# Chunk outputs of a state-space layer straight from the inputs by row-tiled products, without a filter table in DRAM, and the key rows in other accumulator banks than the queries'

## The chip, the core and the metric

The kernel runs on one core of a Trainium2 chip as one program. The metric is the device time of an execution in microseconds. Five engines work side by side, each through its own queue in order: TensorE (PE, its weight loads PEld), VectorE (DVE), ScalarE (ACT), GpSimd (POOL) and SyncE (SP), which here issues DMAs.

## The reference

Two transformer blocks in float32 on 256 tokens of width 1024, with 16 meta tokens ahead of them (272 rows) in the first block. The change touches the first layer's first half alone:

```python
proj = rms_norm(h, norm1_g) @ w_in                  # q 512, k 128, v 128, u 512
attn = sliding_window_attention(q, k, v, ...)       # 8 query heads, 2 key heads, window 128, meta, sinks
ssm  = s5_ssm(u, ...)                               # 32 groups of 16 channels, 64 complex states each
h = h + concat(rms_norm(attn), rms_norm(ssm)) @ w_out
```

`s5_ssm` is a diagonal linear recurrence: s_t = a s_(t-1) + B u_t and y_t = Re(C s_t) + d u_t, then z = gelu(y) and z * sigmoid(z @ glu_w + glu_b). After this half comes the expert layer with product keys (8 heads, 16 of 16384 experts each), and then the second block, with two more layers.

## The kernel before

The program is written as a flow of Python generators over tiles; a planner at compile time puts the instructions of each engine in order by its own estimates, their place in the program and the dependencies. A call `c.after(b, a)` tells it that b must stand behind a on its engine. Each tile of a pool has a tag; tiles of one tag share one buffer (or as many as `bufs` says), and the next tile waits until all uses of the last are over.

PSUM has eight banks in this half: `p` twice, `y`, `o`, `m` twice, `b` twice. Every product of w_in and w_out runs as three fp32r products (`mm3`: high by high, high by low, low by high; lines 1702 to 1704). The weights come through a feed: SP loads a unit of 512 KB into one of five buffers (L89), ScalarE casts the high part (H, L102), and VectorE subtracts to give the low part (Lo, L103; GpSimd for the first four units).

The order of the first half: the rows are normalized and transposed, u is projected into the banks p, p, y, o, and `enter` copies it out by ScalarE (uP), writes it to DRAM (udr) and reads it back as U, 8 steps by 16 channels on 128 partitions. `powers` makes the tables W (six VectorE operations on 2048 columns, ending at L452), `tables` makes rotation tables on GpSimd, and `outputs` makes the output tables G (six VectorE operations on 2304 columns, L590 to L595). Their temporaries share buffers: `tg` has the buffers t0 and t1, and the state inputs st later take t0.

Then two things run interleaved. In the background `kv` projects keys and values (banks p, p, o), normalizes the key rows by 13 small VectorE operations (rstd) and scales them into ks (L285); `q` projects the queries (banks p, p, eight steps of six products); `attention` computes 16 scores (L363, two for each head), adds the mask (L364), takes exponentials (L372), transposes the weights (L392), multiplies by the values (L401, L405) and projects with the first half of w_out. In the foreground `Ssm.run` works in chunks of 8 steps (SJ = 8, 34 chunks):

1. `maps` transposes W into WT (L561). 32 fp32 products of U by WT (L633; each fp32 product is two instructions) give the chunk inputs to the states, which ScalarE copies into st (L638).
2. `response` multiplies bd by G (32 products on four column tiles, L608) to the impulse response K of 8 steps, 16 by 16 for each group. K with zeros in front goes to DRAM (kdr, L616), and eight DMAs (L620) read it back shifted, as a table T of 128 by 128 for each group.
3. VectorE rotates the state inputs (L647 to L650), scans over the chunks (L655), rotates back (L658, L659) and writes S (L667).
4. The chunk outputs, four blocks b of four pairs j of groups, in the banks y, b, y, b:

```python
m = nc.tensor.matmul(y[q:q + 32, o], self.U[:, 2 * j + g, 2:], self.T[:, 2 * j + g], ...)     # L689, g = 0, 1
m = nc.tensor.matmul(y[0:64, o], S[z][:, j]..., self.G[z][:, j, 1:]..., ...)                  # L695, z = 0, 1
```

5. GELU on ScalarE (L699), transposes to zT (L705), and the GLU product (L718), whose weights (`glu`, 1 MB, L351) are loaded once the buffers of the first stage are free.

After step 3 GpSimd zeroes 2048 columns and sends them to `wscr` by four DMAs of 2 MB (L672), behind the last read of T. Two orders by hand bear on the feed: units 11 to 14 (w_out) are loaded behind the last read of T, unit 10 behind the reads of U. The attention weights' transposes stand behind the last L695 (`ylast`). When both halves of the flow are done, `ssm_glu` applies the gate (tanh, L742; L744 to L748) and the second half of w_out follows; then the expert layer begins.

Of the kernel before, what the change touches and what calls it, by code (L numbers as in the profile page):

```python
# [19 lines left out]
FT = mybir.dt.float32  # L20
# [36 lines left out]
CST = {}  # L57
NCST = _cols(CST, [("ident", 128), ("iota", 128), ("bd", 8), ("ones", 1), ("g2", 8), ("tok", 1)])

# [118 lines left out]
def first_half(c):  # L178
# [4 lines left out]
    with ExitStack() as ctx:  # L183
# [50 lines left out]

        up = [c.psum(t) for t in ("p", "p", "y", "o")]
        for k in range(3):
# [14 lines left out]
        ssm.tables()  # L251
        ssm.outputs()

# [9 lines left out]
        def kv():  # L263
            ps = [c.psum(t) for t in ("p", "p", "o")]
            for q in range(2):
                H, Lo = c.feed.take()
                for k2 in range(4):
                    k = 4 * q + k2
                    for i, s, m in ((0, slice(16, 144), 128), (1, slice(144, 272), 128), (2, slice(0, 16), 16)):
                        n = slice(k2 * 256, k2 * 256 + 256)  # L270
                        c.mm3(ps[i][:m, :256], hH[:, k, s], hL[:, k, s], H[:, n], Lo[:, n], k == 0, k == 7)
                    yield 980
            kss = inp.tile([128, 3, 2], FT, name="kss")
            ks = inp.tile([128, 3, 128], FT, name="ks")
            vm = inp.tile([16, 128], FT, name="vm")
            rep = inp.tile([16, 8, 16], FT, name="rep")
            V.memset(kss, 1.0)
            V.tensor_copy(rep, c.ident[:16, None, :16].to_broadcast([16, 8, 16]))
            for i, m in ((0, 128), (1, 128), (2, 16)):
                nc.scalar.activation(ks[:m, i], ps[i][:m, :128], AF.Square)  # L280
                V.tensor_reduce(kss[:m, i], ks[:m, i].rearrange("p (h d) -> p h d", h=2), axis=AX.X, op=OP.add)
                nc.scalar.copy(vr[:, i] if i < 2 else vm, ps[i][:m, 128:256])
            kr = c.rstd(kss.rearrange("p a b -> p (a b)"), 6, 1.0 / 64)
            for i, m in ((0, 128), (1, 128), (2, 16)):
                V.tensor_tensor(ks[:m, i].rearrange("p (h d) -> p h d", h=2), ps[i][:m, :128].rearrange("p (h d) -> p h d", h=2),  # L285
                                kr[:m, 2 * i:2 * i + 2, None].to_broadcast([m, 2, 64]), op=OP.mult)

            def turn():
                p = c.psum("m")
                nc.tensor.transpose(p[:, 0:16], ks[:16, 2], c.ident[:16, :16])  # L290
                for i in range(2):
                    nc.tensor.transpose(p[:, 16 + i * 128:144 + i * 128], ks[:, i], c.ident)
                nc.scalar.activation(kT, p[:, :L], AF.Copy, scale=P1("kg"))

            def spread():
# [137 lines left out]
class Ssm:  # L433
# [106 lines left out]
    def enter(self, up):  # L540

        nc, c, one = self.nc, self.c, self.one
        uP = one.tile([128, 4 * L], FT, tag="uP", name="uP").rearrange("p (a j c) -> p a j c", a=4, j=SJ)
        self.U = U = one.tile([128, 32, SC], FT, name="U")
        for ct in range(4):
            nc.scalar.copy(uP[:, ct].rearrange("p j c -> p c j"), up[ct][:, :L].rearrange("p (c j) -> p c j", j=SJ))
            nc.sync.dma_start(c.udr[ct * 128:(ct + 1) * 128], uP[:, ct])
        src = c.udr.rearrange("(g q) j c -> q j g c", q=16)
        for j in range(SJ):
            m = SJ - 1 - j  # L550
            self.had = [nc.sync.dma_start(U[16 * m:16 * m + 16], src[:, j])]
# [29 lines left out]
    def outputs(self):  # L581
# [8 lines left out]
        for op in (V.tensor_tensor(self.G[0], C[0], a[0], op=OP.mult), V.tensor_tensor(t[0], C[1], a[1], op=OP.mult)):  # L590
            c.after(op, self.wdone)
        V.tensor_tensor(self.G[0], self.G[0], t[0], op=OP.subtract)
        c.after(V.tensor_tensor(self.G[1], C[0], a[1], op=OP.mult), self.wdone)
        V.tensor_tensor(t[1], C[1], a[0], op=OP.mult)
        V.scalar_tensor_tensor(self.G[1], self.G[1], -1.0, t[1], op0=OP.mult, op1=OP.subtract)  # L595

    def response(self, left):


        nc, c, V, P1, one = self.nc, self.c, self.V, self.P1, self.one  # L600
        K = one.tile([128, 4 * L], FT, tag="uP", name="K")[:, :4 * (2 * SJ - 1) * 16].rearrange("p (a m q) -> p a m q", a=4, q=16)
        V.memset(K[:, :, :SJ - 1], 0.0)
        p = c.psum("m")
        for j in range(16):
            q = 32 * (j % 4)
            o = p[q:q + 32, (j // 4) * 128:(j // 4) * 128 + 128]
            for z in range(2):
# [3 lines left out]
                last = m  # L611
        yield
        p4 = p.rearrange("p (a m q) -> p a m q", a=4, m=SJ)
        V.tensor_tensor(K[:, :, SJ - 1], p4[:, :, 0], P1("dk").rearrange("p (a q) -> p a q", a=4), op=OP.add)
        nc.scalar.copy(K[:, :, SJ:], p4[:, :, 1:])
        nc.sync.dma_start(c.kdr.rearrange("(a p) n -> p a n", p=128), K.rearrange("p a m q -> p a (m q)"))  # L616
        self.T = one.tile([128, 4096], FT, tag="T", name="T").rearrange("p (g n) -> p g n", g=32)
        src = c.kdr.rearrange("(g q) n -> q g n", q=16)
        for m in range(SJ):
            t = nc.sync.dma_start(self.T[16 * m:16 * m + 16], src[:, :, 16 * m:16 * m + 128])  # L620
        self.had.append(t)

    def run(self, glu, out):
        nc, c, V, one = self.nc, self.c, self.V, self.one
        yield 8000
        self.maps()

        st = self.temp("s", 0)[:, :2 * 16 * SC].rearrange("p (z j c) -> p z j c", z=2, j=16)
        for j0, n in ((0, 6), (6, 5), (11, 5)):
# [9 lines left out]
            yield 0  # L639
        respond = self.response(left)  # L640
        next(respond)

# [7 lines left out]
        V.tensor_tensor(m1[:, 1], m1[:, 1], m2[:, 0], op=OP.subtract)  # L650
        next(respond, None)
        yield 2000
# [18 lines left out]
        for i in range(4):  # L671
            m = nc.gpsimd.dma_start(c.wscr[:, 32 * i:32 * i + 32].rearrange("p b t -> p (b t)").rearrange("p (a n) -> p a n", n=2048),  # L672
                                    zero[:, None, :].to_broadcast([128, 2, 2048]))
            c.after(m, self.had[1])
        yield 2000
# [5 lines left out]
        for b in range(4):  # L681
            y = c.psum("yb"[b % 2])
            prev = None
            for jj in range(4):
                j = 4 * b + jj
                o = slice(128 * jj, 128 * jj + 128)
                for g in range(2):
                    q = 32 * g
                    m = nc.tensor.matmul(y[q:q + 32, o], self.U[:, 2 * j + g, 2:], self.T[:, 2 * j + g], start=(jj == 0), stop=False,  # L689
                                         tile_position=(0, q), skip_group_check=True)  # L690
                    if prev is not None:
                        c.after(m, prev)
                    prev = m
                for z in range(2):
                    m = nc.tensor.matmul(y[0:64, o], S[z][:, j].rearrange("p g c -> p (g c)"), self.G[z][:, j, 1:].rearrange("p a b -> p (a b)"),  # L695
                                         start=False, stop=(z == 1), skip_group_check=True)
            self.ylast = m
# [4 lines left out]
        for h in range(2):  # L702
            p = c.psum("by"[h])
            for i in range(SJ):
# [5 lines left out]

        for u, i in [(10, 0)] + [(u, 1) for u in range(11, 15)]:
            if u < len(c.feed.issued):
# [930 lines left out]
def body(tc, A, out):  # L1643
# [3 lines left out]
    with ExitStack() as ctx:  # L1647
# [80 lines left out]
        c.udr = tc.dram_tile([512, SJ, SC], FT, name="udr")  # L1728
        c.kdr = tc.dram_tile([512, (2 * SJ - 1) * 16], FT, name="kdr")
        c.ascr = [tc.dram_tile([128, AB, T], FT, name="ascr%d" % i) for i in range(NB // AB)]  # L1730
# [53 lines left out]
def layout(inp):  # L1784
# [18 lines left out]

    cp = np.arange(512).reshape(2, 8, 2, 16).transpose(0, 2, 1, 3).reshape(-1)
    wo = np.concatenate([wo[:512][qp], wo[512:][cp]], 0)
# [15 lines left out]
    for p in range(16):  # L1821
# [19 lines left out]
           (i // 16 == np.arange(8)[None]).astype(f),  # L1841
           np.ones((128, 1), f), col(g["norm2_g"][0], 8), np.arange(128, dtype=f)[:, None]]
    A["pk1"] = np.concatenate(p1 + [z, causal, z, prev, causal], 1)
# [54 lines left out]
```

## Time and profile before

| | us |
|---|---|
| median of 3 runs (lowest, highest) | 1330.38 (1329.16, 1342.03) |
| the profiled execution: time | 1329.63 |
| the profiled execution: span of the trace | 1327.9 |
| TensorE busy | 1260.6 (95%) |
| VectorE busy | 935.7 (70%) |
| ScalarE busy | 648.7 (49%) |
| GpSimd busy | 292.9 (22%) |
| mean granted clock of TensorE | 0.977 of full |

The profile is that of one execution. An engine's busy share is a mean over stages with different limits: the expert layer and the second block fill most of the span, and the stage that the change touches lies in the first 190 us. A row of a timeline has the start, the length from the first start to the last end, the engine, the line, the operation with output and inputs, and the count; in brackets stands the engine's idle time before it and what ended it. The granted clock is 1.00 at 2.4 GHz and 0.50 at 1.2 GHz.

### The profile page before, as it was taken

The numbers are of one execution on the slowest core, as the hardware profiler recorded it, in microseconds if no ns is written. First come the engines' busy times: TensorE is split into PE (matmuls) and PEld (weight loads), VectorE is DVE, ScalarE is ACT, GpSimd is POOL, SyncE is SP. The second block draws the span as 40 slices with busy tenths as digits, with TensorE's granted clock in tenths as the row PEclk, the third lists the DMA queues.
The fourth block names the chain that finished last, engine by engine and source line by source line (L and its number), as shares of the span: only waits on it lengthen the run. The fifth ranks groups of instructions, "written<-read, shape, count | busy, mean of one in ns | idle before, by whom it ended". The sixth has DMA issues, their size and how long they took to land.

```text
span 1327.9 us, 21246 instructions
## 1 busy us (share of the span) xinstructions
PE 1260.6 (95%) x7816; PEld 1092.6 (82%) x7816; DVE 935.7 (70%) x2193; ACT 648.7 (49%) x1119; POOL 292.9 (22%) x201
## 2 busy tenths in 40 slices
PE   4569999999999999999899999999999999999998
PEld 4556789999999999999788788888887778777776
DVE  6973368898988666665588875555557795678854
ACT  4424345545545444444454444444446647455562
POOL 7010000377877777720000000000000001000010
PEclk9886979999999999999899999999999999999999
DMA  5349255688888777798799986656667454563231
GB/s 201 70 58 357 99 168 191 206 224 225 221 232 228 183 203 203 201 354 303 256 309 312 310 266 190 190 188 187 187 187 239 123 162 141 173 219 112 80 113 46
DMA packets 106296, 262.75 MB, mean 198 GB/s; under 512 B 31552, under 2 KB 37056, under 8 KB 103888
## 3 DMA queue, kind: packets, MB, share of 16 engines
q1 hardware_dynamic: 75280, 227.77, 54.9%
q0 software_dynamic: 21696, 16.85, 7.0%
q10 hardware_dynamic: 9216, 16.78, 3.4%
q8 instruction: 61, 1.00, 0.3%
q14 instruction: 43, 0.35, 0.1%
HBM read 232.72 MB, written 28.38 MB: 197 GB/s over the span
## 4 chain that ended last, share of the span: by engine, by line
PE 84%; DVE 6%; ACT 2%; DMA 1%; issue 1%; DVEq 0%; SPq 0%; ACTq 0%
PE ps L890 26%; PE ps L1702 10%; PE ps L1703 10%; PE ps L1704 10%; PE pr L1702 5%; PE pr L1704 5%; PE pr L1703 5%; PE ps L1103 2%; PE m L1295 2%; DVE Lo L103 2%; PE o L1340 2%; PE m L363 1%; PE m L1334 1%; DMA ga<-ascr 1%; ACT H L102 1%
## 5 line engine op out<-in xcount | busy, mean ns | idle before, releaser
L102 ACT CAST H<-w 128x1024 fp32r<-128x1024 f32 (+1 forms) x370 | 386.2, 1045 | 502.3 <-PE ps L1703 193.2
L103 DVE TENSOR_TENSOR Lo<-w,H 128x1024 fp32r<-128x1024 f32 (+1 forms) x366 | 445.2, 1218 | 186.8 <-ACT H L102 186.5
L1702 PE MATMUL ps<-xH,H 128*128 128x256 f32 x1024 | 290.9, 284 | 0.0
L1703 PE MATMUL ps<-xL,H 128*128 128x256 f32 x1024 | 287.8, 281 | 0.0
L1704 PE MATMUL ps<-xH,Lo 128*128 128x256 f32 x1024 | 287.6, 281 | 0.0
L1061 POOL DMA_INDIRECT wscr<-sent x128 | 238.6, 1864 | 219.6 <-DVE act L1038 153.8
L890 PE MATMUL ps<-H,a 128*128 128x512 f32 x1024 | 281.9, 397 | 4.8 <-ACT a L902 3.0
L890 PEld LDWEIGHTS ps<-H,a 128*128 128x128 f32 x1024 | 194.2, 190 | 50.9 <-ACT a L902 3.2
L1702 PEld LDWEIGHTS ps<-xH,H 128*128 128x128 f32 x1024 | 193.1, 189 | 0.0
L1703 PEld LDWEIGHTS ps<-xL,H 128*128 128x128 f32 x1024 | 193.1, 189 | 0.0
L1704 PEld LDWEIGHTS ps<-xH,Lo 128*128 128x128 f32 x1024 | 192.9, 188 | 0.0
L890 PE MATMUL ps<-Lo,a 128*128 128x512 f32 x512 | 161.4, 397 | 0.3 <-DVE Lo L103 0.3
L1382 POOL TENSOR_TENSOR emx<-emx,vz 128x512 f32<-128x512 f32 x2 | 3.5, 1750 | 543.7 <-DVE vz L1228 543.7
L890 PEld LDWEIGHTS ps<-Lo,a 128*128 128x128 f32 x512 | 96.9, 189 | 23.4 <-DVE Lo L103 0.9
L900 DVE TENSOR_TENSOR act<-ga,act 128x256 f32<-128x256 f32 x128 | 47.5, 420 | 25.8 <-DMA ga<-ascr 25.8
L1702 PE MATMUL pr<-H,exH 128*128 128x512 f32 x128 | 52.5, 410 | 1.3 <-ACT exH L1143 1.0
L903 DVE TENSOR_TENSOR a<-act,a 128x256 fp32r<-128x256 f32 x128 | 53.5, 419 | 0.0
L902 ACT CAST a<-act 128x256 fp32r<-128x256 f32 x128 | 51.3, 400 | 2.7 <-DMA ascr<-ga 2.1
L1090 DVE TENSOR_TENSOR o<-cstt,sel 128x512 f32<-128x512 f32 x32 | 22.1, 692 | 43.0 <-PE ps L1103 27.6
L1702 PE MATMUL pr<-H,oxH 128*128 128x512 f32 (+1 forms) x128 | 50.9, 398 | 1.3 <-ACT oxH L1143 1.1
L844 ACT ACTIVATE ga<-ps 128x256 f32<-128x256 f32 x128 | 48.4, 378 | 6.7 <-PE ps L1704 5.5
L1703 PE MATMUL pr<-Lo,exH 128*128 128x512 f32 x128 | 51.4, 402 | 0.0
(493 smaller groups left out, 1918.5 us busy)
## 6 DMA issues: line engine op xcount, KB each, us to landing
w<-in_ut SPq DMA_DIRECT2D x128, 512.0 KB
w<-in_pv SPq DMA_DIRECT2D x128, 512.0 KB
ascr<-ga ACTq DMA_DIRECT2D x64, 256.0 KB
ga<-ascr SPq DMA_DIRECT2D x64, 256.0 KB
w<-in_we SPq DMA_DIRECT2D x32, 512.0 KB
w<-in_wod SPq DMA_DIRECT2D x28, 512.0 KB
wscr<-zero POOLq DMA_DIRECT2D x4, 2048.0 KB
w<-in_wqy SPq DMA_DIRECT2D x16, 512.0 KB
```

What stands on the lines that cost most here:

```text
L102: self.last = self.nc.scalar.copy(H, self.loaded[u])
L103: eng.tensor_sub(Lo, self.loaded[u], H.bitcast(FT))
L844: nc.scalar.activation(ga[:, blk % 2], p[:, :T], AF.Gelu)
L890: nc.tensor.matmul(acc[2 * th + n], a[:, s], b[:, n * 512:(n + 1) * 512], start=first and e == 0, stop=last and e == 2)
L900: V.tensor_tensor(src, ga[:, blk % 2], src, op=OP.mult)
L902: copied = nc.scalar.copy(aH, src)
L903: V.tensor_sub(aL, src, aH.bitcast(FT))
L1061: ins = c.nc.gpsimd.indirect_dma_start(out=c.wscr.rearrange("i b (t o) -> (i b t) o", o=1), out_offset=bass.IndirectOffsetOnAxis(ap=t.bitc ...
L1103: nc.tensor.matmul(p[:, a * 128:(a + 1) * 128], o1[:, a], o2[:, a], start=True, stop=True)
L1702: nc.tensor.matmul(o, ah, bh, start=first, stop=False)
L1703: nc.tensor.matmul(o, ah, bl, start=False, stop=False)
L1704: nc.tensor.matmul(o, al, bh, start=False, stop=last)
```

## The change

- The chunk outputs from the inputs no longer go through a table. `apart` copies uP twice (on ScalarE) into Ub with the channels of every second group zeroed, by a new constant `gm`. `own` multiplies it by K itself: for each of four row blocks a, each step s and each of four 32-row strips b one product, from 32 rows, 64 columns of weights, and 16 (8 - s) moving columns, at tile position (32 b, 0), into the bank b of y, b, b, o. The products have a fixed order, b fastest.
- K keeps only its eight steps, and the zeroing of its front part, kdr, the write and the eight reads of T go.
- The chunk outputs add S by G to the four banks (64 instructions, L695 as before). Groups and channels stand in another order (`cp` in the layout).
- `outputs` is called after `maps`, and the table products stand behind ks (`c.kept`) instead of behind the tables W.
- u is projected into the banks y, o, p, p; keys and values go to the two halves of bank y, and o.
- Both transposes to zT use bank y. The orders behind the reads of T (units 11 to 14 of the feed, the zeros to `wscr`) go.

```diff
-        up = [c.psum(t) for t in ("p", "p", "y", "o")]
+        up = [c.psum(t) for t in ("y", "o", "p", "p")]
...
         ssm.tables()
-        ssm.outputs()
...
         def kv():
-            ps = [c.psum(t) for t in ("p", "p", "o")]
+            both = c.psum("y")
+            ps = [both[:, 0:256], both[:, 256:512], c.psum("o")]
...
-                V.tensor_tensor(ks[:m, i].rearrange("p (h d) -> p h d", h=2), ps[i][:m, :128].rearrange("p (h d) -> p h d", h=2),
+                c.kept = V.tensor_tensor(ks[:m, i].rearrange("p (h d) -> p h d", h=2), ps[i][:m, :128].rearrange("p (h d) -> p h d", h=2),
...
-            c.after(op, self.wdone)
+            c.after(op, c.kept)
         V.tensor_tensor(self.G[0], self.G[0], t[0], op=OP.subtract)
-        c.after(V.tensor_tensor(self.G[1], C[0], a[1], op=OP.mult), self.wdone)
+        c.after(V.tensor_tensor(self.G[1], C[0], a[1], op=OP.mult), c.kept)
...
+    def apart(self):
+
+        nc, c = self.nc, self.c
+        self.Ub = self.one.tile([128, 4096], FT, tag="T", name="Ub")[:, :4 * SJ * 64].rearrange("p (a j g c) -> p a j g c", a=4, j=SJ, g=2)
+        for g in range(2):
+            nc.scalar.activation(self.Ub[:, :, :, g].rearrange("p a j c -> p (a j) c"), self.uP[:, :, :, 2:].rearrange("p a j c -> p (a j) c"),
+                                 AF.Copy, scale=c.cst("gm")[:, g:g + 1])
...
-        K = one.tile([128, 4 * L], FT, tag="uP", name="K")[:, :4 * (2 * SJ - 1) * 16].rearrange("p (a m q) -> p a m q", a=4, q=16)
-        V.memset(K[:, :, :SJ - 1], 0.0)
+        self.K = K = one.tile([128, 4 * L], FT, tag="uP", name="K")[:, :4 * SJ * 16].rearrange("p (a m q) -> p a m q", a=4, q=16)
...
-        nc.sync.dma_start(c.kdr.rearrange("(a p) n -> p a n", p=128), K.rearrange("p a m q -> p a (m q)"))
-        self.T = one.tile([128, 4096], FT, tag="T", name="T").rearrange("p (g n) -> p g n", g=32)
-        src = c.kdr.rearrange("(g q) n -> q g n", q=16)
-        for m in range(SJ):
-            t = nc.sync.dma_start(self.T[16 * m:16 * m + 16], src[:, :, 16 * m:16 * m + 128])
-        self.had.append(t)
...
+    def own(self):
+
+        nc, c = self.nc, self.c
+        self.y = [c.psum(t) for t in "ybbo"]
+        prev = None
+        for a in range(4):
+            for s in range(SJ):
+                for b, y in enumerate(self.y):
+                    r = slice(32 * b, 32 * b + 32)
+                    m = nc.tensor.matmul(y[0:64, 128 * a + 16 * s:128 * a + 128], self.Ub[r, a, s].rearrange("p g c -> p (g c)"),
+                                         self.K[r, a, :SJ - s].rearrange("p m q -> p (m q)"), start=(a == 0 and s == 0), stop=False,
+                                         tile_position=(32 * b, 0), skip_group_check=True)
+                    if prev is not None:
+                        c.after(m, prev)
+                    prev = m
+            yield 0
...
         self.maps()
+        self.outputs()
+        self.apart()
...
-        respond = self.response(left)
-        next(respond)
+        self.response(left)
+        yield from self.own()
...
         for b in range(4):
-            y = c.psum("yb"[b % 2])
...
+            y = self.y[b]
+            for a in range(4):
+                j = 4 * a + b
                 for z in range(2):
...
-            p = c.psum("by"[h])
+            p = c.psum("y")
...
-        for u, i in [(10, 0)] + [(u, 1) for u in range(11, 15)]:
+        for u, i in [(10, 0)]:
```

## Rows read from the trace of the kernel before

**Rows 1.** Page, the chain that ended last: share of the span by engine.

```profile
PE 84%; DVE 6%; ACT 2%; DMA 1%; issue 1%; DVEq 0%; SPq 0%; ACTq 0%
```

**Rows 2.** Stretches: length, busy us (instructions) of each engine, clock, DMA share, GB/s.

```profile
49.35:71.40 22.05, 5.36 (x42) 4.60 (x41) 21.68 (x29) 3.76 (x8) 0.00 (x0) 0.70 0.01 2
71.40:80.18 8.78, 8.78 (x76) 8.09 (x79) 0.01 (x1) 3.00 (x10) 0.00 (x0) 0.78 0.00 0
80.18:94.64 14.46, 12.22 (x93) 9.09 (x83) 14.28 (x17) 4.21 (x6) 1.85 (x2) 1.00 0.72 95
...
99.67:114.47 14.80, 14.77 (x41) 9.35 (x41) 7.28 (x33) 6.05 (x20) 0.14 (x1) 0.50 1.12 275
114.47:131.44 16.97, 16.97 (x130) 9.96 (x129) 3.86 (x10) 9.69 (x25) 0.00 (x0) 0.85 1.01 424
131.44:151.74 20.30, 19.06 (x132) 16.21 (x131) 3.11 (x6) 6.29 (x15) 0.00 (x0) 1.00 0.31 128
```

**Rows 3.** Timeline of TensorE, 52 to 82 us.

```profile
52.18 2.58 PE L633 MATMUL b<-U,WT 128*128 128x68 f32 x22
71.09 0.80 PE L1702 MATMUL p<-H,hH 128*128 128x512 f32 x1 [16.32 <-DVE ks L285]
...
73.81 2.12 PE L633 MATMUL b<-U,WT 128*128 128x68 f32 x12
...
76.06 3.46 PE L633 MATMUL b<-U,WT 128*128 128x68 f32 x30
79.44 2.03 PE L608 MATMUL m<-G,bd 128*32 128x128 f32 x64
```

**Rows 4.** Timeline of VectorE, 49 to 95 us.

```profile
49.26 2.55 DVE L590 TENSOR_TENSOR G<-pk,A 128x2304 f32<-128x2304 f32 x1
...
62.74 2.55 DVE L595 SCALAR_TENSOR_TENSOR G<-G,tg 128x2304 f32<-128x2304 f32 x1
65.21 1.22 DVE L103 TENSOR_TENSOR Lo<-w,H 128x1024 fp32r<-128x1024 f32 x1
66.34 0.65 DVE L281 TENSOR_REDUCE kss<-ks 128x2 f32<-128x128 f32 x3
...
80.18 1.29 DVE L647 TENSOR_TENSOR m<-s,R 128x1088 f32<-128x1088 f32 x1 [8.77 <-ACT s L638]
...
91.82 2.79 DVE L667 TENSOR_TENSOR S<-m,m 64x512 f32<-64x512 f32 x4
```

**Rows 5.** Timeline of ScalarE, 59 to 123 us.

```profile
59.31 0.66 ACT L638 COPY s<-b 64x204 f32<-64x204 f32 x2 [6.34 <-DVE G L592]
...
122.01 1.28 ACT L699 ACT_TABLE_LOAD   x1
```

**Rows 6.** Timeline of TensorE, 92 to 132 us.

```profile
92.00 0.40 PE L1704 MATMUL p<-H,hL 128*128 128x512 f32 x1
99.67 1.94 PE L327 MATMUL m<-cstt,xs 128*128 128x128 f32 x8 [7.27 <-DVE xs L320]
101.54 12.99 PE L363 MATMUL m<-kT,qT 64*128 64x144 f32 x32
...
124.05 0.41 PE L689 MATMUL y<-T,U 128*32 128x128 f32 x4
124.39 0.65 PE L695 MATMUL y<-G,S 128*64 128x128 f32 x4
124.97 0.41 PE L689 MATMUL y<-T,U 128*32 128x128 f32 x4
...
131.44 0.71 PE L705 MATMUL b<-cstt,zc 64*128 64x64 f32 x8
```

**Rows 7.** Short stretches around the two turns of the granted clock.

```profile
96.00:97.00 1.00, 0.00 (x0) 0.00 (x0) 0.93 (x5) 0.00 (x0) 0.67 (x2) 0.50 1.26 95
...
119.50:120.00 0.50, 0.50 (x6) 0.23 (x4) 0.17 (x1) 0.47 (x3) 0.00 (x0) 0.91 1.05 418
```

**Rows 8.** Timeline of SyncE's DMA queue, the load of GLU's weights.

```profile
103.41 0.33 SPq L351 DMA_DIRECT2D glu<-in_glu  x1
```

More of the change, by code (lines that the diff above doesn't have):

```diff
@@ L57 @@
 CST = {}
-NCST = _cols(CST, [("ident", 128), ("iota", 128), ("bd", 8), ("ones", 1), ("g2", 8), ("tok", 1)])
+NCST = _cols(CST, [("ident", 128), ("iota", 128), ("bd", 8), ("ones", 1), ("g2", 8), ("tok", 1), ("gm", 2)])
 class Ctx:
@@ L270, in kv @@
                         n = slice(k2 * 256, k2 * 256 + 256)
-                        c.mm3(ps[i][:m, :256], hH[:, k, s], hL[:, k, s], H[:, n], Lo[:, n], k == 0, k == 7)
+                        o = ps[i][:m, :256]
+                        a = nc.tensor.matmul(o, hH[:, k, s], H[:, n], start=(k == 0 and i != 1), stop=False, skip_group_check=True)
+                        if k == 0 and i == 1:
+                            c.after(a, head)
+                        head = a
+                        nc.tensor.matmul(o, hH[:, k, s], Lo[:, n], start=False, stop=False, skip_group_check=True)
+                        nc.tensor.matmul(o, hL[:, k, s], H[:, n], start=False, stop=(k == 7), skip_group_check=True)
                     yield 980
@@ L547, in enter @@
             nc.sync.dma_start(c.udr[ct * 128:(ct + 1) * 128], uP[:, ct])
+        self.uP = uP
         src = c.udr.rearrange("(g q) j c -> q j g c", q=16)
@@ L611, in response @@
                 last = m
-        yield
         p4 = p.rearrange("p (a m q) -> p a m q", a=4, m=SJ)
-        V.tensor_tensor(K[:, :, SJ - 1], p4[:, :, 0], P1("dk").rearrange("p (a q) -> p a q", a=4), op=OP.add)
-        nc.scalar.copy(K[:, :, SJ:], p4[:, :, 1:])
-        nc.sync.dma_start(c.kdr.rearrange("(a p) n -> p a n", p=128), K.rearrange("p a m q -> p a (m q)"))
-        self.T = one.tile([128, 4096], FT, tag="T", name="T").rearrange("p (g n) -> p g n", g=32)
-        src = c.kdr.rearrange("(g q) n -> q g n", q=16)
-        for m in range(SJ):
-            t = nc.sync.dma_start(self.T[16 * m:16 * m + 16], src[:, :, 16 * m:16 * m + 128])
-        self.had.append(t)
+        V.tensor_tensor(K[:, :, 0], p4[:, :, 0], P1("dk").rearrange("p (a q) -> p a q", a=4), op=OP.add)
+        nc.scalar.copy(K[:, :, 1:], p4[:, :, 1:])
+    def own(self):
[13 more added lines that the diff above has]
+            yield 0
     def run(self, glu, out):
@@ L650, in run @@
         V.tensor_tensor(m1[:, 1], m1[:, 1], m2[:, 0], op=OP.subtract)
-        next(respond, None)
         yield 2000
@@ L671, in run @@
         for i in range(4):
-            m = nc.gpsimd.dma_start(c.wscr[:, 32 * i:32 * i + 32].rearrange("p b t -> p (b t)").rearrange("p (a n) -> p a n", n=2048),
+            nc.gpsimd.dma_start(c.wscr[:, 32 * i:32 * i + 32].rearrange("p b t -> p (b t)").rearrange("p (a n) -> p a n", n=2048),
                                     zero[:, None, :].to_broadcast([128, 2, 2048]))
-            c.after(m, self.had[1])
         yield 2000
@@ L681, in run @@
         for b in range(4):
-            y = c.psum("yb"[b % 2])
[L683 to L693, printed above, removed]
+            y = self.y[b]
+            for a in range(4):
+                j = 4 * a + b
                 for z in range(2):
-                    m = nc.tensor.matmul(y[0:64, o], S[z][:, j].rearrange("p g c -> p (g c)"), self.G[z][:, j, 1:].rearrange("p a b -> p (a b)"),
-                                         start=False, stop=(z == 1), skip_group_check=True)
+                    m = nc.tensor.matmul(y[0:64, 128 * a:128 * a + 128], S[z][:, j].rearrange("p g c -> p (g c)"),
+                                         self.G[z][:, j, 1:].rearrange("p a b -> p (a b)"), start=False, stop=(z == 1), skip_group_check=True)
             self.ylast = m
@@ L1728, in body @@
         c.udr = tc.dram_tile([512, SJ, SC], FT, name="udr")
-        c.kdr = tc.dram_tile([512, (2 * SJ - 1) * 16], FT, name="kdr")
         c.ascr = [tc.dram_tile([128, AB, T], FT, name="ascr%d" % i) for i in range(NB // AB)]
@@ L1802, in layout @@
     wo = g["w_out"][0]
-    cp = np.arange(512).reshape(2, 8, 2, 16).transpose(0, 2, 1, 3).reshape(-1)
+    cp = np.arange(512).reshape(4, 2, 2, 2, 16).transpose(1, 3, 2, 0, 4).reshape(-1)
     wo = np.concatenate([wo[:512][qp], wo[512:][cp]], 0)
@@ L1841, in layout @@
            (i // 16 == np.arange(8)[None]).astype(f),
-           np.ones((128, 1), f), col(g["norm2_g"][0], 8), np.arange(128, dtype=f)[:, None]]
+           np.ones((128, 1), f), col(g["norm2_g"][0], 8), np.arange(128, dtype=f)[:, None],
+           (i // 16 % 2 == np.arange(2)[None]).astype(f)]
     A["pk1"] = np.concatenate(p1 + [z, causal, z, prev, causal], 1)
```

## Prediction

> **What bounds the kernel now.** I read the chain that ended last first: 84% of the span is TensorE [rows 1], so what counts is where TensorE waits or does work that could go. The table by stretches [rows 2] shows one place, between 49 and 152 us. From 49.35 to 71.40 VectorE is busy 21.68 of 22.05 us and TensorE 5.36; from 71.40 to 80.18 it is the other way round (VectorE 0.01); from 99.67 to 151.74 TensorE is busy throughout, and the chain runs on it. TensorE's own order of time says why [rows 3]: after eleven state-input products (L633, 22 instructions) the next instruction in its queue is the first query product, which waits 16.32 us for the last scaling of the key rows (ks, L285), because queries and keys share the two "p" banks. VectorE reaches ks so late because the six table products of outputs() stand ahead of it, from 49.26 (L590) to 65.29 (L595) [rows 4]. Behind the query product wait the other L633s; VectorE sits 8.77 us before L647 for ScalarE's copies of them (st) [rows 4]. From 80.18 VectorE works without a gap until S at 94.61 (L667), so those 8.8 us are on the path.
>
> The second place is 99.67 to 131.44 [rows 6]: query transposes and the 16 scores (L363), 14.8 us at a granted clock of 0.50 (1.2 GHz), then the chunk outputs: 64 instructions L689 (filter table) and 64 L695 (states), 16.97 us, and only then the transposes L705 and the attention work. The scores depend on ks and the queries, not on the chunk outputs, so the attention work stands behind 17 us that it does not need.
>
> **The change part by part.** The sum is made on the profiled execution: 1329.63 us, its span 1327.9 and 1.7 around it, 0.75 below the median 1330.38.
>
> *Key rows in banks y and o, G behind ks.* VectorE's work from 49.35 to L647 stays (six Gs at 2.5, three cuts Lo, sums, rsqrt, ks), less the zeroing of K; only ks goes ahead of G. So G ends near 71.5 as before, and L647 could begin there: 8.8 us gained at most. What is next: st lies in the buffer of the first table temporary (ScalarE's first copy waited 6.34 us for G L592 [rows 5]). That comes free after the third or fourth G, ks + 7.4 to 10; ks itself ends at 55 to 56.5 (49.35, two or three cuts of 1.15, and the 3.6 us that sums, rsqrt and ks take from 66.34 on without the cut and the zeroing between them), so 63 to 66. Two of six groups of L633 are ready by then; the other four cost 10 instructions each, 1.15 us at the fast pace (30 in 3.46), 1.77 at the slow one (12 in 2.12) [rows 3], so st is complete at 68 to 73. I take 7 us gained, 5 to 8.8 for the range. The query products (48 instructions) fill TensorE from 51 on, as soon as cuts are there.
>
> *The filter table.* Its write and eight reads leave the SP queue, and its 64 matmul instructions L689 go. In their place own() has 128 products, 256 instructions on four 32-row tiles into four banks. No instruction before has this form. The nearest row is L608, four column tiles side by side: 64 in 2.03 us, 32 ns each [rows 3], 8.1 us for 256. From above, one after another: L633, 68 columns wide, 115 ns, 29 us; at its slow pace, 177 ns, 45 us. I take 10 us: it is four tiles as in L608, and the moving width averages 72 columns against 128, but weights are 64 wide against 32. Its slot: G ends near 71.5, L608 2 us, K 0.5 to 1, so it starts near 75.5 and S comes at 94.6 - 7 = 87.6: 12 us, in which TensorE has only the last query products (3 us). So it is costed at nothing; its cover is VectorE's scan chain, and beyond 12 us each microsecond is one on the path. A gain below nothing is excluded, because the path up to S is VectorE's.
>
> *The chunk outputs.* Without a table to wait for, L695 is ready with S, at 87.6, while VectorE still normalizes the queries (5.1 us; TensorE idles 7.27 us here now [rows 6]). L695 costs 0.58 us per four at full clock, 9.3 in all. 5.1 go into that gap. The 17 us between scores and attention work go: -17. The remaining 4.2 meet the score stretch. At full clock that stretch is half of 14.8, 7.4, plus 4.2 = 11.6, -3; if the clock falls as it begins, 14.8 + 4.2, +4; if it is at half level from 87 on, 11.5 of L695 remain, +11.5. In the rows TensorE stopped at 92.4, the clock was 0.50 by 96, and it came back only at 119.5, five microseconds after L689 began [rows 2, 6, 7]. Now TensorE stops nowhere between 87 and the scores, which speaks for full; the scores at half level never brought it back, which speaks against. I take +1.
>
> The chunk outputs alternate with the table products, and each four L689 take 0.34 us (85 ns each) where L608, in one run, takes 32 [rows 3, 6]. The Trainium skill (TensorEngine Tiling (Array Packing), Key Properties) says that a change of tiling mode drains the engine, and these rows agree. By that rule L695 in one run would go at L633's 115 ns, 7.4 instead of 9.3 us, and the forecast would be 1.9 us lower; against the change, own() would pay a drain wherever a query product is put between its tiles. I keep the pace of the row.
>
> *Small terms.* GELU now comes ahead of the exponentials, so ScalarE loads its table once more before the tanh: 1.28 us [rows 5], on the path there (cut, tanh, z): +1.3, from 0. The loads of w_out no longer wait for the table's reads, so one or two of its cuts Lo (1.15 us each [rows 4]) can fall into VectorE's chain ahead of S: +1.2, 0 to 2.3. Both L705 halves use one bank: +0.5. GLU's weights are asked for at 103.4 now [rows 8] and about 9 us earlier then, beside 8.4 MB of zeros at some 420 GB/s [rows 2] (20 us): there by 110 to 113. They are needed when the scores end (about 107), but attention work that does not need them lies beside: nothing, up to +3. The copies of Ub are two on an idle ScalarE: nothing. Four banks are now held from own() to GELU; their next users (attention's o, the L718 sums) come after GELU anyway: nothing.
>
> The work from 131.44 to 151.74 stays 20.3 us; up to 4 of it (L705, L718) may slip into gaps of the scores, which I leave for the range. What follows is TensorE's and moves up as a whole. Sum: -7 - 17 + 1 + 1.3 + 1.2 + 0.5 = -20: 1309.6.
>
> **The rivals.** (a) *Order kept.* TensorE's order is a planner's. It may leave L695 behind the scores, as it does now, although only the table forced it. Then 87.6 + 5.1 + 14.8 = 107.5 for the scores and about 12 us of L695 (five of them at half clock), end 119.5 + 2.5 of small terms: 9.5 us gained, 1320. For it: now all 32 score instructions stand ahead of the first L689. Against: the table's reads end close to there, so the planner had a reason.
> (b) *Row tiles one after another, full clock.* own() takes 29 us: 75.5 + 29 + 9.3 + 7.4 to 14.8 = 121 to 128.5 for the end of scores and outputs, plus 3: 0 to 7 us gained, 1323 to 1330.
> (c) *Row tiles one after another at half clock: slower.* 45 us: 75.5 + 45 + 9.3 + 14.8 = 144.6, 13 us later than 131.44: 1343. It decides from 32 us (124 ns an instruction) with scores at half clock, 39 us at full. For it: TensorE may pause between st and own(), and small tiles may not bring the clock up. Against: the 64 L608 ran at 32 ns.
> (d) *The queries don't move.* The cuts Lo come late, or the planner puts query products elsewhere, the 8.8 us stay, and what is gained behind is eaten by half clock (+11.5): 1325 to 1329.
> The Trainium skill (TensorE: Matmul & The Clock Gate, Part 3) states that weight loads overlap running matmuls only where row groups differ, and gives 3.07 times for four row tiles. By it own() would be 29 / 3.07 = 9.4 us, an estimate; no run here shows it, and (b) and (c) would fall.
>
> **How the numbers follow.** Forecast (14 to 33 us gained, 1297 to 1316) 0.60, (a) 0.15, (b) 0.10, (c) 0.07, (d) 0.08. The low end takes 8.8, the -3, no small terms and half of the 4: 1300. The high end must take in (a) and part of (b): 1326. A measurement of this kernel can tell 1%, 13 us, from no change: faster is the forecast and the lower half of (a), 0.68; slower is (c) and a little of (d), 0.09; the rest 0.23.
>
> **What would show it.** Right: no wait of a query product for ks; L647 at 72 to 75; own() in 8 to 14 us, ended before S; L695 without L689 between, begun before the query transposes; a granted clock above 0.5 in the scores; L705 at 107 to 112; the attention part's first product (L1702 on aH) near 130 (it ends the last stretch of 20.3 us, at 151.74, now), and the rest unchanged in length. Wrong: own() over 30 us; L695 behind the scores; TensorE waiting for st, K or GLU's weights; scores at half clock with L695 between them.

## The result, and the profile after

| | before | after |
|---|---|---|
| median (lowest to highest), us | 1334.93 (1328.49 to 1342.71), 7 runs | 1319.33 (1316.64 to 1323.83), 7 runs |
| ratio of the two, 95% interval | | 0.9895 [0.9865, 0.9925] |
| the profiled execution, us | 1329.63 | 1322.22 |
| its span, mean granted clock | 1327.9, 0.977 | 1320.4, 0.978 |

The kernel is faster by just over 1%. The forecast was 1310 (1309.6 in the sum); the time lies inside the range (1299 to 1326), 9.3 us above the forecast and above the band of 1297 to 1316 that the forecast gave for its own mechanism. Measured again beside the experiments, the same kernel gave 1317.45 and a ratio of 0.9850 [0.9826, 0.9874]. Between the two profiled executions lie only 7.4 us: the one of before, 1329.63, is among the fastest of its kernel. The sum of the prediction was made on it, so the miss is taken apart on the profiled executions below.

Of the page, the chain that ended last, which answers to [rows 1]:

```profile
PE 85%; DVE 9%; DMA 3%; ACT 2%; issue 1%; POOL 0%; SPq 0%; DVEq 0%; ACTq 0%
```

VectorE and DMA have more of the chain than before (6% and 1%). The next views show where. From the key rows on, line numbers are 6 to 25 higher than before; the operations keep their names.

The timeline of VectorE, to be read beside [rows 4]:

```profile
49.33 2.29 DVE L458 TENSOR_TENSOR W<-W,tw 128x2048 f32<-128x2048 f32 x1
...
57.39 2.56 DVE L601 TENSOR_TENSOR tg<-pk,A 128x2304 f32<-128x2304 f32 x1 [1.24 <-PE m L568]
59.87 0.16 DVE L1732 TENSOR_TENSOR rs<-ri 128x6 f32<-128x6 f32 x1
59.94 1.22 DVE L103 TENSOR_TENSOR Lo<-w,H 128x1024 fp32r<-128x1024 f32 x1
...
63.08 0.27 DVE L291 TENSOR_TENSOR ks<-o,rs 16x128 f32<-16x128 f32 x1
63.27 2.54 DVE L597 TENSOR_TENSOR G<-pk,A 128x2304 f32<-128x2304 f32 x1
...
70.68 2.54 DVE L599 TENSOR_TENSOR G<-G,tg 128x2304 f32<-128x2304 f32 x1
...
83.48 1.29 DVE L672 TENSOR_TENSOR m<-s,R 128x1088 f32<-128x1088 f32 x1 [1.97 <-ACT s L663]
...
94.56 2.80 DVE L691 TENSOR_TENSOR S<-m,m 64x512 f32<-64x512 f32 x4
```

A table product (L601) and a cut stand in the middle of the small operations that lead to ks, so ks ends at 63.35 and not at 55 to 56.5. (The tables W, done at 51.62, 2.3 us later than before, account for most of the rest of that delay.) The subtraction L599, which frees the buffer that st needs, is the last but one of the six. The state products therefore come late, as the timelines of ScalarE and TensorE show (beside [rows 5] and [rows 3]):

```profile
73.31 1.34 ACT L663 COPY s<-b 64x204 f32<-64x204 f32 x4 [4.83 <-DVE G L599]
```

```profile
47.14 0.63 PE L1716 MATMUL p<-H,hH 128*128 128x512 f32 x2
...
66.52 0.40 PE L1718 MATMUL p<-H,hL 128*128 128x512 f32 x1
66.75 2.79 PE L658 MATMUL b<-U,WT 128*128 128x68 f32 x24
74.01 8.80 PE L658 MATMUL b<-U,WT 128*128 128x68 f32 x40 [4.47 <-ACT s L663]
```

The wait of 16.32 us for ks in [rows 3] is gone: the 48 query products run from 47.14 to 66.9. But the first rotation of the state inputs (m) begins at 83.48, against 80.18, and S ends at 97.36, against 94.61.

From there on, TensorE's timeline answers to [rows 6]:

```profile
96.10 0.66 PE L709 MATMUL y<-G,S 128*64 128x128 f32 x2 [2.88 <-DVE S L691]
97.51 3.22 PE L709 MATMUL y<-G,S 128*64 128x128 f32 x14 [0.76 <-DVE S L691]
100.53 2.85 PE L709 MATMUL b<-G,S 128*64 128x128 f32 x16
103.30 1.09 PE L333 MATMUL m<-cstt,xs 128*128 128x128 f32 x8
104.33 1.96 PE L709 MATMUL b<-G,S 128*64 128x128 f32 x16
106.22 0.52 PE L369 MATMUL m<-kT,qT 64*128 64x144 f32 x4
...
112.32 0.68 PE L719 MATMUL y<-cstt,zc 64*128 64x64 f32 x8
117.29 1.22 PE L732 MATMUL b<-zT,glu 128*128 128x256 f32 x2 [4.29 <-DMA glu<-in_glu]
118.44 1.28 PE L369 MATMUL m<-kT,qT 64*128 64x272 f32 x4
...
142.94 0.50 PE L1716 MATMUL p<-H,aH 128*128 128x512 f32 x1 [0.68 <-ACT aH L425]
```

The chunk outputs L709 begin before the query transposes (L333), and 48 of their 64 instructions stand ahead of the first score product (L369). They are done by 109.4; they ended at 131.44 before. Then comes a new wait, 4.29 us for GLU's weights. Twelve score products (L369, 272 columns) stand behind the GLU products in TensorE's order, though they need no GLU weights. In the chain of waits the load is the longest piece of the stage:

```profile
105.29 11.96 DMA glu<-in_glu
```

Stretches (columns as in [rows 2]): the granted clock is 1.00 in the first half of the scores and 0.51 behind the wait, for the twelve that are left of the second half.

```profile
72.00:84.00 12.00, 9.99 (x64) 9.83 (x68) 8.89 (x8) 5.74 (x14) 0.00 (x0) 0.50 0.38 117
...
93.00:96.00 3.00, 0.22 (x10) 0.12 (x4) 2.94 (x6) 1.28 (x1) 0.00 (x0) 0.94 0.02 5
96.00:100.00 4.00, 3.15 (x14) 2.81 (x15) 3.83 (x8) 0.00 (x0) 2.25 (x2) 0.50 0.00 0
...
104.00:112.00 8.00, 7.66 (x64) 6.25 (x62) 3.09 (x17) 2.44 (x5) 0.00 (x0) 1.00 1.01 369
112.00:116.00 4.00, 1.00 (x11) 0.58 (x8) 1.76 (x8) 3.66 (x13) 0.00 (x0) 1.00 1.02 424
116.00:124.00 8.00, 6.71 (x18) 3.02 (x18) 1.86 (x8) 1.31 (x7) 0.00 (x0) 0.51 1.01 428
```

The product of the attention's first half with w_out (L1716 on aH) begins at 142.94, 8.8 us earlier than before. What follows lasts 1320.4 - 142.94 = 1177.5 us, against 1176.2.

### The profile page after: what moved, and what is told of

Same layout as the page of the kernel before. It is cut to its first block, busy times and chain, and to the rows that moved or that the text cites. A ratio compares the mean times of both kernels' runs of the same rounds, so it can differ in the third digit from the quotient of the medians.

```text
span 1320.4 us, 21626 instructions
## 1 busy us (share of the span) xinstructions
PE 1262.1 (96%) x8008; PEld 1100.2 (83%) x8008; DVE 936.9 (71%) x2192; ACT 651.8 (49%) x1122; POOL 296.3 (22%) x201
## 4 chain that ended last, share of the span: by engine, by line
PE 85%; DVE 9%; DMA 3%; ACT 2%; issue 1%; POOL 0%; SPq 0%; DVEq 0%; ACTq 0%
PE ps L904 25%; PE ps L1716 10%; PE ps L1717 10%; PE ps L1718 10%; PE pr L1716 5%; PE pr L1718 5%; PE pr L1717 5%; DVE Lo L103 2%; PE ps L1117 2%; PE m L1309 2%; PE o L1354 2%; DMA ga<-ascr 1%; PE m L1348 1%; DMA glu<-in_glu 1%; PE b L732 1%
## 5 line engine op out<-in xcount | busy, mean ns | idle before, releaser
L1716 PE MATMUL ps<-xH,H 128*128 128x256 f32 x1024 | 290.9, 284 | 0.0
L1716 PEld LDWEIGHTS ps<-xH,H 128*128 128x128 f32 x1024 | 193.1, 189 | 0.0
L1716 PE MATMUL pr<-H,exH 128*128 128x512 f32 x128 | 52.5, 410 | 1.3 <-ACT exH L1157 1.0
L1716 PE MATMUL pr<-H,oxH 128*128 128x512 f32 (+1 forms) x128 | 50.9, 398 | 1.3 <-ACT oxH L1157 1.1
```

The costliest lines, as they stand in the source:

```text
L1716: nc.tensor.matmul(o, ah, bh, start=first, stop=False)
```

## The experiments

Three times tell the kernels apart: the end of S, the start of the first attention product on aH, and the rest of the span behind that. Each ratio is to the before of its own series, measured beside it: 1334.93 for after, 1335.71 for after_again and the next three, 1333.08 for own_alone to before_again, 1331.86 for the last two. The last three columns come from one profiled execution each.

| run | median us | ratio to before, 95% | S ends | aH product | rest |
|---|---|---|---|---|---|
| before (first profile) | 1334.93 | | 94.61 | 151.74 | 1176.2 |
| after (first profile) | 1319.33 | 0.9895 [0.9865, 0.9925] | 97.36 | 142.94 | 1177.5 |
| after_again | 1317.45 | 0.9850 [0.9826, 0.9874] | 95.01 | 139.20 | 1177.8 |
| zeros_behind_glu | 1309.27 | 0.9816 [0.9787, 0.9845] | 95.41 | 133.41 | 1171.1 |
| tables_behind_ks | 1312.60 | 0.9823 [0.9789, 0.9857] | 89.70 | 132.67 | 1174.1 |
| both_orders | 1301.92 | 0.9746 [0.9721, 0.9771] | 89.54 | 126.73 | 1173.3 |
| own_alone | 1327.83 | 0.9958 [0.9929, 0.9987] | 99.08 | 154.09 | 1174.9 |
| banks_alone | 1337.89 | 1.0025 [0.9999, 1.0050] | 92.24 | 155.62 | 1173.8 |
| strip_by_strip | 1330.33 | 0.9977 [0.9955, 0.9999] | 94.64 | 152.52 | 1174.1 |
| before_again | 1335.19 | 1.0001 [0.9975, 1.0027] | 96.58 | 157.89 | 1175.9 |
| own_zeros | 1320.80 | 0.9900 [0.9832, 0.9967] | 98.14 | 149.65 | 1175.3 |
| before_zeros | 1334.32 | 1.0022 [0.9997, 1.0047] | 95.21 | 152.36 | 1177.1 |

The rest lies between 1171.1 and 1177.8, while the start of the aH product moves by 31 us: what the change does shows ahead of that product. About half of the spread of the rest comes from one stretch. Where TensorE stops for the gate (tanh), some 15 to 18 us behind the start of the aH product, the granted clock falls to 0.50, and it stays there for 6.8 us in six of the twelve profiles and for 13.7 us in the other six; the longer one costs some 3.4 us more. The kernel before has one of each, 167.37 to 181.03 in the first profile and 172.86 to 179.69 in before_again, so the change is not needed for it; what decides it is not shown. So two profiled executions can differ by that much without any edit.

**after_again**, the changed kernel, no edit.

> The changed kernel once more, to compare the three below with on the same chip: 1316 to 1324 us, 10 to 16 below the kernel before. If only the profiled execution counted (7.4 us between the two profiled executions), it would be 5 to 9 below.

1317.45, 18.3 us below the kernel before of its series, more than the 10 to 16 that I expected and far from the rival's 5 to 9. This execution waited 4.06 us for GLU's weights, at 114.64: the wait is no accident of one profile. S ended 2.35 us earlier than in the first; of that, 1.3 us is the tables W, done at 50.3 against 51.62.

**zeros_behind_glu**, the stores of zeros to `wscr` put behind the load of GLU's weights.

```diff
-            nc.gpsimd.dma_start(c.wscr[...]..., zero[...]...)
+            c.zeros.append(nc.gpsimd.dma_start(c.wscr[...]..., zero[...]...))
...
-            nc.sync.dma_start(glu, A["glu"][:, 0])
+            c.gload = nc.sync.dma_start(glu, A["glu"][:, 0])
...
+        for m in c.zeros:
+            c.tc.add_manual_dep(m.ins, c.gload.ins.name, ...)
```

> The four zeroing DMAs to wscr (8.4 MB) wait for the load of GLU's weights; nothing else is changed. Theory: in the changed kernel that load lies behind the zeros (issued 105.3, landed 117.3), TensorE stands 4.3 us for it and works at half clock behind it for some 8 us more. Without that: no wait of the GLU product for its weights, the scores at full clock, 6 us less than the changed kernel (4 to 9). Rival: the wait only stands where the exponentials or the scores would have been waited for, and less than 2 us are gained. Second rival: the zeros come later and collide with the loads of w_out or of the expert layer: no gain or a loss.

8.2 us less than after_again by the medians, inside the 4 to 9 that I expected; two of its six runs (1316.41 and 1316.85) lie among those of after_again. The weights, asked for at 103.42, had landed by 110.17, when GpSimd's first store began: at most 6.75 us against 11.96. TensorE no longer waits, and the scores between the GLU products run at full clock:

```profile
110.44 0.68 PE L720 MATMUL y<-cstt,zc 64*128 64x64 f32 x8
111.06 0.70 PE L735 MATMUL b<-zT,glu 128*128 128x256 f32 x2
111.68 0.73 PE L369 MATMUL m<-kT,qT 64*128 64x272 f32 x4
...
121.41 1.12 PE L407 MATMUL o<-vb,PT 128*128 128x512 f32 x2
```

From the first GLU product to the first L407 it takes 10.35 us; in the first profile after it took 13.76 (117.29 to 131.05). So the wait of 4.3 brings 3.4 of half clock with it, 7.7 in all; in after_again it is 4.06 and 2.2 (12.56 us from the first GLU product to the first L407). The two profiled executions, after_again and this one, differ by 12.5 us: 5.8 of it lie ahead of the aH product, where the edit shows, and 6.7 behind it, 3.3 of these in the stretch at the gate.

**tables_behind_ks**, two of the table products put behind the first subtraction, so that none of the six can stand ahead of ks and t0 comes free earlier.

```diff
-        V.tensor_tensor(self.G[0], self.G[0], t[0], op=OP.subtract)
-        c.after(V.tensor_tensor(self.G[1], C[0], a[1], op=OP.mult), c.kept)
-        V.tensor_tensor(t[1], C[1], a[0], op=OP.mult)
+        g0 = V.tensor_tensor(self.G[0], self.G[0], t[0], op=OP.subtract)
+        c.after(V.tensor_tensor(self.G[1], C[0], a[1], op=OP.mult), g0)
+        c.after(V.tensor_tensor(t[1], C[1], a[0], op=OP.mult), g0)
```

> All table products G stand behind ks, and the fourth and fifth behind the subtraction that frees st's buffer. Theory: ks ends near 57 instead of 63, the buffer is free near 66 instead of 73, st is complete near 77 instead of 83.5, and S comes 4 to 6 us earlier; of that 3 to 6 us reach the end. Rival: the zeros and the load of GLU's weights, 20 us of transfer behind S and the queries, set the time; TensorE then waits longer for the weights, and less than 2 us are gained.

4.9 us less than after_again by the medians. That alone is not clear of the noise: its six runs spread from 1304.87 to 1318.65, those of after_again from 1315.06 to 1318.88. In the trace S ends 5.3 us earlier. VectorE's timeline now has the order that the prediction took for granted:

```profile
56.93 0.27 DVE L291 TENSOR_TENSOR ks<-o,rs 16x128 f32<-16x128 f32 x1
57.13 2.54 DVE L597 TENSOR_TENSOR G<-pk,A 128x2304 f32<-128x2304 f32 x1
...
63.20 2.54 DVE L599 TENSOR_TENSOR G<-G,tg 128x2304 f32<-128x2304 f32 x1
...
76.53 1.27 DVE L672 TENSOR_TENSOR m<-s,R 128x1088 f32<-128x1088 f32 x1
```

The first rotation no longer waits for st. The wait for GLU's weights is still there (4.25 us, at 108.63): load and stores both come forward with S.

**both_orders**, the two edits together.

> The last two edits together. Theory: they add up, 9 to 13 us below the changed kernel (near 1308). Rival (the load sets the time): as the first alone, 4 to 7. If TensorE's clock falls in the scores all the same, 5 to 8.

1301.92, the fastest of all, 15.5 us below after_again, where the two edits alone give 8.2 and 4.9. That is more than the 9 to 13 that I expected. Beside zeros_behind_glu, the same order of the tables is worth 7.4 us. TensorE's clock stays at 1.00 from 96 to 132, and TensorE no longer waits for the weights.

**own_alone**, the products from the inputs without the other banks and with the table products G where they were before.

```diff
-        up = [c.psum(t) for t in ("y", "o", "p", "p")]
+        up = [c.psum(t) for t in ("p", "p", "y", "o")]
...
         ssm.tables()
+        ssm.outputs()
...
-            c.after(op, c.kept)
+            c.after(op, self.wdone)
...
         self.maps()
-        self.outputs()
```

`kv` is that of the kernel before.

> Only the chunk outputs change (own() in place of the filter table); banks, and the place of the table products G, as before. Theory: what was gained came from here. The key rows stay late (ks near 71, S near 95), but nothing of the chunk outputs stands between scores and attention work: 8 to 14 us below the kernel before. Rival: the queries' early place is needed to use it, and it is worth less than half: 0 to 6.

5.3 us gained by the medians, 5.6 by the ratio: my 8 to 14 was wrong, the rival right. The filter table is gone, yet ks ends at 72.7, so the query products stand around own() and among the chunk outputs, the last of them at 107, and the query transposes come at 114.04, against 99.67 in [rows 6]. The freed time is spent waiting for the queries; the attention part is no earlier than before (154.09).

**banks_alone**, the other banks and the late G with the filter table kept.

```diff
-        up = [c.psum(t) for t in ("p", "p", "y", "o")]
+        up = [c.psum(t) for t in ("y", "o", "p", "p")]
...
-        ssm.outputs()
...
-            c.after(op, self.wdone)
+            c.after(op, c.kept)
...
         self.maps()
+        self.outputs()
```

`kv` is that of the change; kdr, the table T and its products stay.

> Only the banks of keys and queries and the place of G change; the filter table goes through DRAM as before. Theory: S comes no earlier (st waits for its buffer until near 73), so nothing is gained: -2 to +3 us against the kernel before. Rival: the 16 us wait that goes is worth 5 to 8 us less.

Nothing gained, as I expected, but not for my reason: S does come earlier, by 2.4 us (92.24). The scores come 2.6 us earlier, but now TensorE waits for the table behind them, where the kernel before had just enough cover:

```profile
98.96 12.99 PE L369 MATMUL m<-kT,qT 64*128 64x144 f32 x32
117.25 0.64 PE L696 MATMUL y<-T,U 128*32 128x128 f32 x4 [5.29 <-DMA T<-kdr]
```

**strip_by_strip**, own() with the same 256 instructions, but the eight steps of one strip before the next strip.

```diff
-            for s in range(SJ):
-                for b, y in enumerate(self.y):
+            for b, y in enumerate(self.y):
+                for s in range(SJ):
```

> The changed kernel with the products of own() ordered strip by strip (eight in a row on one 32-row strip) instead of strips in turn; the same products. Theory: strips in turn run side by side, 256 instructions in 5.8 us; in a row they take 60 to 115 ns each, 15 to 29 us, end at 103 to 117 instead of 93, and the whole is 5 to 20 us slower than the changed kernel. Rival: the instructions are short by themselves, and order makes no difference (under 2 us).

The stretch of own() in the two kernels, its own instructions alone (first fence: the changed kernel; second: strip by strip; the columns are length, TensorE, weight loads, clock, DMA share, GB/s):

```profile
87.40:93.20 5.80, 5.30 (x256) 4.99 (x256) 1.00 0.02 6
```

```profile
84.70:115.00 30.30, 29.34 (x256) 29.23 (x256) 0.52 0.56 230
```

21 ns an instruction against 115, and the granted clock falls to half 1 us after the strips begin (84.77). The gain of the change is nearly gone (0.9977), although the scores behind run at full clock. So this is where the rivals (b) and (c) live: the order decides, not the size of the tiles. Each strip writes to a bank of its own, so eight products in a row on one strip also go to one bank; whether the strip or the bank makes them slow, no run separates.

**before_again**, the kernel before, no edit.

> The kernel before once more with a second profile: no difference, 1328 to 1342. If the span is near the upper end, the two profiles show where it varies; if the theory that the transfers of the filter table and the zeros together vary is right, in the stretch from 80 to 140 us.

Its profile has what the first one did not, a wait of the GLU product in the kernel before:

```profile
138.29 0.77 PE L718 MATMUL b<-zT,glu 128*128 128x256 f32 x2 [2.31 <-DMA glu<-in_glu]
```

**own_zeros**, own_alone with the zeros behind the load.

> The part of the change around the chunk outputs alone (as in own_alone), with the zeros to wscr put behind the load of GLU's weights. In own_alone TensorE waited 3.59 us for these weights at 126.96 and ran 120 to 132 at 0.50. My theory, that the chunk outputs also need the early queries: the query products still stand behind own() and among the chunk outputs, so the query transposes stay at 112 to 115; the wait and most of the half clock behind it go, 5 to 8 us: 1319 to 1323, ratio 0.988 to 0.992, some 10 us above zeros_behind_glu's ratio of 0.9816. The rival, that only the GLU weights held own_alone back and early queries add nothing: ratio 0.980 to 0.984, as zeros_behind_glu.

Ratio 0.9900, in the middle of what I expected, but its interval reaches into the rival's 0.980 to 0.984. Its four runs are two pairs, 1314.55 and 1314.72, and 1326.87 and 1329.74; the profile is of 1326.87. It shows no wait for the weights, the query transposes still late (113.03), and the clock still at 0.50 from 120 to 132. No trace shows one of the faster pair. Against zeros_behind_glu (0.9816) the early queries would be worth 11 us by the median and 7 by the faster pair (1314.6 to 1331.86 is 0.987).

**before_zeros**, the kernel before with the same edit.

> The kernel before, whose zeros to wscr wait for the load of GLU's weights too. My theory: in the kernel before the weights are there at about the time they are needed (no wait in one profiled execution, 2.31 us in another), so moving the zeros takes away 0 to 4 us: ratio 0.997 to 1.000, and with it the upper part of the spread of its times. The rival, that the stores of zeros cost every kernel here the same 8 us, whatever the order of the chunk outputs: ratio 0.993 to 0.995, and then that part of zeros_behind_glu's gain has nothing to do with the change.

Ratio 1.0022 [0.9997, 1.0047]: nothing gained, and the spread (1330.42 to 1340.18) stays. The rival falls: the 8.2 us belong to the changed kernel, where the GLU product comes 16.5 us earlier (117.29 against 133.80). My side guess falls too: the spread of before is not that wait.

## Why the prediction was right, and where its sizes were off

In the main the mechanism held. The query products no longer wait for ks; L709 has no table products between its instructions and begins before the query transposes; own() ends ahead of S; the transposes to zT (L719) begin at 109.73, inside 107 to 112; the rest is unchanged but for 1.3 us. Other signs failed: the first rotation (L647 before, L672 now) came at 83.48 and not at 72 to 75, the aH product at 142.94 and not near 130. And of my signs of being wrong, TensorE waited for st (4.47 us before 74.01) and for GLU's weights (4.29 us before 117.29), and twelve of the score products ran at 0.51 between the GLU products.

That the time is inside the range is in part luck. The range reached to 1326 because it took in (a), and the measured 1319.33 is next to the 1320 of (a), whose order did not come. Between the profiled executions, on which the sum was made, 7.4 of the 20 us came; by the medians it is 15.6, because the median before, 1334.93, lies above the 1329.63 that I started from.

Forecast and measurement are told apart by two sums, one up to S and one behind it.

**Up to S: the term that was mis-sized.** I took -7 for the key rows and queries, and +1.2 for the cuts, -5.8 together; the first profile shows +2.75, the second +0.4. Tables W that were done 2.3 and 1.0 us later account for that much; what is left of the term is about nothing (+0.5 and -0.6). The step that failed is "only ks goes ahead of G", with ks at 55 to 56.5 and the buffer free at 63 to 66. The diff orders only three of the six operations behind ks; L601 was free, and the planner put it first and the subtraction that frees t0 last but one. From the end of W to ks it is 11.7 us here and 7.0 in tables_behind_ks. tables_behind_ks shows what the order was worth: ks at 57.2, t0 free at 65.7, S 4.9 us earlier than before and 5.8 earlier if W (0.9 later) is counted out, which is what the two terms make together. The split was off even there: m begins at 76.53, 3.65 us earlier than before (4.5 without W's delay), less than the 5 to 8.8 that I gave for it, because two cuts and a sum stand just ahead of it; behind m, with one cut less, it is 13.2 us to S against 14.4.

**Behind S: near, by two errors against each other.** From the end of S to the aH product it was 57.13 us. I took 15.5 off (-17 + 1 + 0.5): 41.6. Measured: 45.58 and 44.2. The GLU weights, which I had at "nothing, up to +3", cost 7.7 in the first profile and 6.3 in the second. I had them asked for 9 us earlier than 103.41 [rows 8]; but the load follows ScalarE's copies of the query transposes, these follow S, and with S late it was issued at 105.29, behind 8.4 MB of zeros that start 2 us after S. And "attention work that does not need them lies beside" was true of the work, not of its place in the queue. Without the wait the stretch is 38.0 (zeros_behind_glu) and 37.2 (both_orders), 3.6 and 4.4 less than I had: about what I had priced for scores at full clock (-3 where I took +1), and the scores of these two kernels run at 1.00.

**The rest.** No load of ScalarE's table stands between the exponentials' at 112.33 and the tanh at 157.93, so the +1.3 is zero. The rest is 1.3 longer all the same: right behind the aH product the clock was at 0.50 from 143.40 to 146.81, which cost some 1.6 us and which no other profile shows. Together: 8.55 up to S, 4.0 behind it: the 12.5 us between 1322.22 and 1309.6.

**own().** 5.7 us, from 87.49 to 93.22, 5.30 of it busy, where I took 10. Nothing hangs on it: S ended 4 us later. The same 256 instructions take 29.34 us strip by strip, at a clock of 0.52. For both at half level: in both_orders 92 of them began between 80 and 83 us, with the clock at 0.50, 33 ns each, against 115 (243 between 86 and 114 in strip_by_strip); about 3.5 times, an estimate, since the widths are not quite the same. The Trainium skill (TensorE: Matmul & The Clock Gate, Part 3) states 3.07 times for four row tiles with wider products; these two traces show somewhat more. My 9.4 us by that page was too long mainly through its base, L633's 115 ns at full clock, which these smaller products need at half.

**L695 in one run.** 16 in 1.89 us (104.33 to 106.22), 118 ns each, against 145 in [rows 6] between table products. The Trainium skill (TensorEngine Tiling (Array Packing), Key Properties) says that a change of mode drains the engine; the trace agrees, and at full clock the 1.9 us that I left out were there to take. At half clock it is 216 ns (14 in 3.02 from 97.51), against 262 between table products in the kernel before (four in 1.05 from 115.04): TensorE stood idle for 2.88 us before 96.10, and the clock was 0.50 from 96 to 102. I had expected no stop there; own() was done before S.

**The rivals.** (a) is out by its order, though not by its time: the planner put most of L709 ahead of the scores. (b) and (c) need serial tiles, which the order of the loops prevents; strip_by_strip is their case, and its 1330.33 lies at the upper end of the 1323 to 1330 that (b) gave for 29 us. The 13 us of loss that (c) forecast needed 45 us for own() and did not come. (d), queries that do not move, is own_alone: 1327.83, inside its 1325 to 1329. The two parts of the change need each other: alone they are worth some 5 us and nothing, together 15.6 to 18.3.

**What stays open:** why the kernel before spreads from 1327 to 1343 (its two profiles differ by 6 us at the aH product, and by 3.4 the other way at the gate), and what own_zeros does in its faster pair.

## What to carry to other kernels

Count a freed stretch only up to the next thing that hangs on it, and read the order of each queue: a wait moves to the first instruction in order that needs something late, and everything behind it waits too, needed or not. Where a forecast rests on an order ("only ks goes ahead"), look whether a dependency forces it; if the planner is free, price the other order: two orders forced by a few lines brought 15.5 us here, as much as the change. A small load that is needed soon should be issued ahead of large stores that nobody waits for; it pays only where something stands waiting for that load, as before_zeros (nothing gained) suggests.

## What the runs showed of the hardware that was not expected

- Four row tiles of 32 rows and 64 columns, taken in turn over four banks, go at 21 ns an instruction at full clock and 33 at half; the same instructions with eight in a row on one strip and bank at 115 ns, at half clock.
- In strip_by_strip TensorE is busy in the record without a gap, and yet the granted clock, 1.00 when these products began (84.77), was 0.50 by 86.0 and stayed there until they were over. In both_orders, with the tiles in turn, it fell to 0.50 at 79.88, as own() began, and was back at 1.00 from 83.30, during own(). The stretches of strip_by_strip, all engines:

```profile
85.00:85.50 0.50, 0.50 (x8) 0.50 (x7) 0.50 (x2) 0.00 (x0) 0.00 (x0) 1.00 0.00 0
85.50:86.00 0.50, 0.50 (x11) 0.50 (x11) 0.50 (x2) 0.00 (x0) 0.00 (x0) 0.80 0.00 0
86.00:86.50 0.50, 0.50 (x7) 0.50 (x6) 0.50 (x2) 0.00 (x0) 0.00 (x0) 0.50 0.00 0
```

- 1 MB of weights took 11.96 us to land beside the stores of zeros, and at most 6.75 us ahead of them.
